# Two products of one weight tile in one 512-column matmul, in the memory stage of a decoder layer

## The chip, the cores and the metric

The program runs on one core of one Trainium2 chip. The time is device time in microseconds (us), from launch to end. Five engines with queues of their own matter: PE (TensorE, matrix multiply; its weight loads are shown as PEld), ACT (ScalarE), DVE (VectorE), POOL (GpSimd) and SP, which issues most DMAs. Each queue is worked off in the order in which the program was written out. Matmuls write into PSUM banks of 512 columns of 32 bits.

## The reference

One decoder layer on 512 tokens of width 2048: token mixing (retention and sliding-window attention), cross-attention into 256 memory tokens, gated MLP, each followed by a layer norm of the scaled residual sum. Only the cross-attention matters here:

```python
def memory_cross_attention(x, mem, wq, wkv, wo):
    q = (x @ wq).reshape(B, S, XA_HEADS, XA_HD)          # 4 heads of 512
    k, v = jnp.split(mem @ wkv, 2, axis=-1)              # 256 memory tokens
    logits = jnp.einsum('bshd,bmhd->bhsm', q, k) * XA_HD ** -0.5
    p = jax.nn.softmax(logits, axis=-1)
    return jnp.einsum('bhsm,bmhd->bshd', p, v).reshape(B, S, D_MODEL) @ wo
```

## The kernel before

All values are 32-bit floats. Each matrix is split into a high part and a low part (`split`: ACT casts the high part, DVE subtracts it to get the low part), and each product is made of three matmuls that add into one bank: high by high, low by high, high by low (`mm3`, lines 96 to 98).

The stage `memory()` comes first in the program and needs only the memory tokens and weights. Since keys and values are small, it folds them into the weights beside them. For each of four heads it runs

- `proj` twice: keys and values of the head, four weight chunks each. A chunk (1 MB, 128 rows by 2048 columns) is loaded into `raw` by a DMA on SP, split in two halves of 1024 columns into `whi` and `wlo` (four buffers each, so two chunks), and 16 weight tiles of each chunk multiply the memory tokens (`mh`, `ml`, 256 columns each) into a bank `psW`. The bank is split into `kvh` and `kvl`.
- the loop over `fq`: four chunks of `xa_q`, 16 tiles each, multiply the keys into banks `psT`. Eight tiles of a half chunk fill one bank (two results of 256 columns side by side), and ACT copies the whole bank to `ao`, which a DMA writes to a scratch tensor.
- `as_block`: four chunks of `xa_o` are multiplied by tiles of the values, into banks `psA` and `psB`; DVE copies them to `oo`.

There are two banks of each of the four kinds. A tile that takes a buffer over waits for the last reader of the tile that had it. The order of the instructions on each engine is not that of the source: a scheduler orders them when the program is built and writes one list for each engine. Two lines set what the change touches:

```python
def split(self, hi, lo, src, eng=None):
    self.nc.scalar.copy(hi, src)
    (eng or self.nc.vector).tensor_tensor(lo, src, hi.bitcast(F32), op=ALU.subtract)
```

Of the kernel before, what the change touches and what calls it, by code (L numbers as in the profile page):

```python
# [10 lines left out]
F32 = mybir.dt.float32  # L11
F32R = mybir.dt.float32r
AF = mybir.ActivationFunctionType
ALU = mybir.AluOpType
# [3 lines left out]
P = 128  # L18
D = 2048
S = 512  # L20
ML = 256
KT = D // P
# [14 lines left out]
class Layer:  # L37
# [128 lines left out]
    def memory(self):  # L166
        nc, I = self.nc, self.I
        with ExitStack() as c:
            mp = self.pool(c, "mem")
            mh = [mp.tile([P, 4, ML], F32R, name=f"mh{g}") for g in range(4)]  # L170
            ml = [mp.tile([P, 4, ML], F32R, name=f"ml{g}") for g in range(4)]
            ms = lambda k, cc: (mh[k // 4][:, k % 4, cc], ml[k // 4][:, k % 4, cc])
            stage = lambda: mp.tile([P, 2048], F32, name=self.n("stg"), tag="stg", bufs=2)
            raws = [stage() for _ in range(2)]
            first = self.st.tile([P, 2048], F32, name=self.n("raw"), tag="raw", bufs=3)

            def piece(i):
                k = slice(2 * i, 2 * i + 2)
                r = raws[i // 4].rearrange("p (k s) -> p k s", k=8)[:, 2 * i % 8:2 * i % 8 + 2]
                nc.sync.dma_start(r, I["memT"][:, k, :])  # L180
                kk = slice(2 * i % 4, 2 * i % 4 + 2)
                self.split(mh[i // 2][:, kk], ml[i // 2][:, kk], r)

            pre = []
            for h in range(2):
                piece(4 * h)
                c = slice(h * 1024, (h + 1) * 1024)
                nc.sync.dma_start(first[:, c], I["xa_k"][0][:, c])
                hi, lo = self.halves()
                self.split(hi, lo, first[:, c])  # L190
                pre.append((hi, lo))
                for i in range(1, 4):
                    piece(4 * h + i)
            def proj(name, h, pre=None):
                hi = mp.tile([P, 4, ML], F32R, name=self.n("kvh"), tag="kvh", bufs=2)
                lo = mp.tile([P, 4, ML], F32R, name=self.n("kvl"), tag="kvl", bufs=2)
                for q in range(4):
                    if pre and q == 0:
                        ps = self.bank("W")
                        self.ws_mm(ps, pre, ms, slice(0, ML))  # L200
                    else:
                        ps = self.ws(I[name][4 * h + q], ms, ML)
                    self.split(hi[:, q], lo[:, q], ps[:, :ML])
                return lambda k, cc: (hi[:, k, cc], lo[:, k, cc])

            self.swa_tables(mp)
            for h in range(XH):
                ks = proj("xa_k", h, pre if h == 0 else None)
                vs = proj("xa_v", h)
                if h == 1:  # L210
                    for g in range(4):
                        r = stage().rearrange("p (k s) -> p k s", k=4)
                        nc.sync.dma_start(r, I["xT"][:, 4 * g:4 * g + 4, :])
                        self.split(self.ah[g], self.al[g], r)
                for fq in range(4):
                    o = mp.tile([P, 4, ML], F32, name=self.n("ao"), tag="ao", bufs=2)
                    for hf, (hi, lo) in enumerate(self.chunk(I["xa_q"][4 * h + fq])):
                        ps = self.bank("T")
                        for i in range(2):
                            for k in range(4):  # L220
                                c = slice((4 * i + k) * P, (4 * i + k + 1) * P)
                                self.mm3(ps[:, i * ML:(i + 1) * ML], (hi[:, c], lo[:, c]), ks(k, slice(0, ML)),
                                         k == 0, k == 3)
                        nc.scalar.copy(o[:, 2 * hf:2 * hf + 2], ps.rearrange("p (i m) -> p i m", i=2))
                    nc.sync.dma_start(self.asc[h // 2][fq][:, :, h % 2 * ML:(h % 2 + 1) * ML], o)
                if h == 0:
                    self.swa_spread()
                for cb in range(4):
                    def done(m, a):
                        o = mp.tile([P, S], F32, name=self.n("oo"), tag="oo", bufs=2)  # L230
                        nc.vector.tensor_copy(o, a)
                        k = 2 * h + m
                        nc.sync.dma_start(self.osc[cb][k // 4][:, k % 4], o)

                    self.as_block([I["xa_o"][4 * h + cb]], vs, 512, 2, done, 4, "AA" if cb % 2 else "BB")


    def swa_tables(self, mp):
# [675 lines left out]
```

## Time and profile before

| | |
|---|---|
| runs | 2770.05, 2772.43, 2772.47 us; median 2772.43 us |
| profiled execution, its own time | 2770.75 us |
| its span, first to last instruction | 2769.0 us, so 1.75 us lie around it |
| PE busy | 2724.3 us, 98% of the span, 14402 matmuls |
| weight loads (PEld) | 85%, DVE 59%, ACT 34%, POOL 9% |
| granted clock | 0.993 of full speed on average |

The memory stage is the first 383 us or so. A matmul's busy time overlaps that of the next one, so the step from one matmul's start to the next one's is the measure of what it costs, and an idle time in front of one says what PE waited for.

### The profile page before, as it was taken

The page shows a single profiled execution, that of the slowest core. Times are in us where ns is not written, and L with a number is a line of the kernel's source. Part 1 is how long each engine was busy: PE and PEld are TensorE (multiplying, and loading weights), DVE is VectorE, ACT ScalarE, POOL GpSimd, SP SyncE. Part 2 cuts the span into 40 slices and gives each one's busy share as a digit, 9 for nine tenths or more (in the row PEclk, how much of TensorE's full clock was granted, in tenths as well). Part 3 has the DMA queues.
Part 4 walks back from the last instruction along what each step waited for, and adds up shares of the span by engine and source line. Part 5 has one row for each costly group of instructions (what it writes and reads, how often), then busy time and mean ns, then how long its engine had stood idle before and what let it go on. Part 6 is the DMA issues. An engine that isn't in the chain of part 4 may idle for free.

```text
span 2769.0 us, 35144 instructions
## 1 busy us (share of the span) xinstructions
PE 2724.3 (98%) x14402; PEld 2348.0 (85%) x14402; DVE 1635.8 (59%) x2344; ACT 945.6 (34%) x1304; POOL 262.1 (9%) x244
## 2 busy tenths in 40 slices
PE   8999999999999999999999999999999999999997
PEld 7999988898989988978888888888888888888876
DVE  6554545675344434554667667666666766666677
ACT  5444434442212322322433333333333333333331
POOL 0000001222111000260450000000000000000003
PEclk9999999999999999999999999999999999999998
DMA  8776672323222343132232223332223233322331
GB/s 320 244 243 208 226 232 79 95 74 97 99 88 96 122 152 125 43 126 93 95 111 98 103 92 107 107 107 92 97 102 107 92 106 107 107 100 99 107 122 61
DMA packets 70178, 337.68 MB, mean 122 GB/s; under 512 B 7504, under 2 KB 22272, under 8 KB 33536
## 3 DMA queue, kind: packets, MB, share of 16 engines
q1 hardware_dynamic: 63168, 320.89, 33.8%
q10 hardware_dynamic: 6848, 14.54, 1.6%
q8 instruction: 113, 1.85, 0.3%
q14 instruction: 49, 0.40, 0.1%
HBM read 311.27 MB, written 26.23 MB: 122 GB/s over the span
## 4 chain that ended last, share of the span: by engine, by line
PE 61%; DVE 2%; POOL 1%; ACT 0%; issue 0%; DMA 0%; DVEq 0%; ACTq 0%; POOLq 0%
PE psT L97 6%; PE psT L96 6%; PE psT L98 6%; PE psW L97 6%; PE psW L98 6%; PE psW L96 6%; PE psA L96 5%; PE psA L98 5%; PE psA L97 5%; PE psB L98 4%; PE psB L96 4%; PE psB L97 4%; PE psT L497 0%; POOL y L461 0%; DVE y L632 0%
## 5 line engine op out<-in xcount | busy, mean ns | idle before, releaser
L74 DVE TENSOR_TENSOR wlo<-raw,whi 128x1024 fp32r<-128x1024 f32 x512 | 643.8, 1260 | 848.2 <-ACT whi L73 846.9
L73 ACT CAST whi<-raw 128x1024 fp32r<-128x1024 f32 x512 | 537.4, 1051 | 1269.5 <-PE psW L97 572.6
L96 PE MATMUL psW<-ah,whi 128*128 128x512 f32 (+1 forms) x1136 | 443.3, 390 | 0.7 <-ACT ah L73 0.7
L98 PE MATMUL psW<-ah,wlo 128*128 128x512 f32 (+1 forms) x1136 | 442.1, 389 | 0.0
L97 PE MATMUL psW<-al,whi 128*128 128x512 f32 (+1 forms) x1136 | 441.3, 388 | 0.0
L96 PE MATMUL psT<-ah,whi 128*128 128x512 f32 (+1 forms) x720 | 276.7, 384 | 0.0
L97 PE MATMUL psT<-al,whi 128*128 128x512 f32 (+1 forms) x720 | 276.7, 384 | 0.0
L98 PE MATMUL psT<-ah,wlo 128*128 128x512 f32 (+1 forms) x720 | 276.7, 384 | 0.0
L96 PEld LDWEIGHTS psW<-ah,whi 128*128 128x128 f32 x1136 | 214.5, 189 | 44.1 <-ACT ah L73 1.2
L97 PEld LDWEIGHTS psW<-al,whi 128*128 128x128 f32 x1136 | 214.5, 189 | 43.7 <-issue 0.6
L96 PE MATMUL psA<-whi,ah 128*128 128x256 f32 (+1 forms) x800 | 245.8, 308 | 5.6 <-ACT xp L525 3.0
L98 PEld LDWEIGHTS psW<-ah,wlo 128*128 128x128 f32 x1136 | 214.6, 189 | 42.4
L97 PE MATMUL psA<-wlo,ah 128*128 128x256 f32 (+1 forms) x800 | 245.0, 306 | 0.0
L98 PE MATMUL psA<-whi,al 128*128 128x256 f32 (+1 forms) x800 | 244.8, 306 | 0.0
L96 PEld LDWEIGHTS psA<-whi,ah 128*128 128x128 f32 x800 | 153.7, 192 | 13.7 <-ACT xp L525 3.4
L97 PEld LDWEIGHTS psA<-wlo,ah 128*128 128x128 f32 x800 | 153.8, 192 | 6.6
L98 PEld LDWEIGHTS psA<-whi,al 128*128 128x128 f32 x800 | 153.7, 192 | 6.5
L98 PEld LDWEIGHTS psT<-ah,wlo 128*128 128x128 f32 x720 | 135.3, 188 | 26.8
L96 PEld LDWEIGHTS psT<-ah,whi 128*128 128x128 f32 x720 | 135.3, 188 | 26.8
L97 PEld LDWEIGHTS psT<-al,whi 128*128 128x128 f32 x720 | 135.3, 188 | 26.8
L96 PE MATMUL psW<-mh,whi 128*128 128x256 f32 x512 | 146.1, 285 | 3.0 <-ACT whi L73 3.0
L98 PE MATMUL psW<-mh,wlo 128*128 128x256 f32 x512 | 146.0, 285 | 2.3 <-DVE wlo L74 2.3
(307 smaller groups left out, 4759.6 us busy)
## 6 DMA issues: line engine op xcount, KB each, us to landing
raw<-in_ffn_up SPq DMA_DIRECT2D x88, 1024.0 KB, 4.9
raw<-in_w_in SPq DMA_DIRECT2D x44, 1024.0 KB, 5.0
raw<-in_ffn_down SPq DMA_DIRECT2D x44, 1024.0 KB, 4.9
raw<-in_xa_v SPq DMA_DIRECT2D x16, 1024.0 KB, 5.2
raw<-in_xa_q SPq DMA_DIRECT2D x16, 1024.0 KB, 4.9
raw<-in_xa_o SPq DMA_DIRECT2D x16, 1024.0 KB, 5.9
raw<-in_w_o SPq DMA_DIRECT2D x16, 1024.0 KB, 4.9
raw<-in_xa_k SPq DMA_DIRECT2D x15, 1024.0 KB, 7.1
```

Of the source, the lines that this page charges most:

```text
L73: self.nc.scalar.copy(hi, src)
L74: (eng or self.nc.vector).tensor_tensor(lo, src, hi.bitcast(F32), op=ALU.subtract)
L96: mm(ps, a[0], b[0], start=start, stop=False)
L97: mm(ps, a[0], b[1], start=False, stop=False)
L98: return mm(ps, a[1], b[0], start=False, stop=stop)
```

## The change

High and low parts lie side by side in one tile (`mt` for the memory tokens, `kv` for keys and values, 2 by 256 columns). A weight tile's high part multiplies both by one matmul of 512 columns, and its low part multiplies the high part by one of 256 columns. So the bank's left half holds two of the three products, its right half the third, and `both` adds the halves: ACT copies the right half to SBUF, DVE adds the left one to it. In `proj` the sum goes to a new tile `kt` before it is split. In the `fq` loop one result now fills a bank, so that a bank changes after 8 matmuls (4 tiles), where it changed after 24 (8 tiles).

```diff
-            mh = [mp.tile([P, 4, ML], F32R, name=f"mh{g}") for g in range(4)]
-            ml = [mp.tile([P, 4, ML], F32R, name=f"ml{g}") for g in range(4)]
+            mt = [mp.tile([P, 4, 2, ML], F32R, name=f"mt{g}") for g in range(4)]
+            ms = lambda k: mt[k // 4][:, k % 4]
...
+            def wide(ps, hi, lo, m, start, stop):
+
+                nc.tensor.matmul(ps, hi, m.rearrange("p i m -> p (i m)"), start=start, stop=False)
+                nc.tensor.matmul(ps[:, :ML], lo, m[:, 0], start=False, stop=stop)
+
+            def both(out, ps):
+
+                nc.scalar.copy(out, ps[:, ML:])
+                nc.vector.tensor_tensor(out, ps[:, :ML], out, op=ALU.add)
...
+                    hv = pre if pre and q == 0 else self.chunk(I[name][4 * h + q])
+                    ps = self.bank("W")
+                    for k in range(KT):
+                        hi, lo = hv[k // 8]
+                        w = slice((k % 8) * P, (k % 8 + 1) * P)
+                        wide(ps, hi[:, w], lo[:, w], ms(k), k == 0, k == KT - 1)
+                    t = mp.tile([P, ML], F32, name=self.n("kt"), tag="kt", bufs=2)
+                    both(t, ps)
+                    self.split(kv[:, q, 0], kv[:, q, 1], t)
...
                     for hf, (hi, lo) in enumerate(self.chunk(I["xa_q"][4 * h + fq])):
-                        ps = self.bank("T")
                         for i in range(2):
+                            ps = self.bank("T")
                             for k in range(4):
                                 c = slice((4 * i + k) * P, (4 * i + k + 1) * P)
-                                self.mm3(ps[:, i * ML:(i + 1) * ML], (hi[:, c], lo[:, c]), ks(k, slice(0, ML)),
-                                         k == 0, k == 3)
-                        nc.scalar.copy(o[:, 2 * hf:2 * hf + 2], ps.rearrange("p (i m) -> p i m", i=2))
+                                wide(ps, hi[:, c], lo[:, c], ks[:, k], k == 0, k == 3)
+                            both(o[:, 2 * hf + i], ps)
```

The scheduler's lists move with it. In the `fq` loop of the first head, ACT's list before alternates the cast of a weight half (L73, `whi`) and the copy of a whole bank (L224); the number behind a name only tells one tile from another.

```order
L73 CAST whi_778<-raw_776 128x1024
L224 COPY ao_647<-psT_658 128x512
L73 CAST whi_782<-raw_776 128x1024
L224 COPY ao_647<-psT_684 128x512
L73 CAST whi_842<-raw_840 128x1024
L224 COPY ao_711<-psT_722 128x512
L73 CAST whi_846<-raw_840 128x1024
```

ACT's list of the changed kernel at the same place (L200 is the copy in `both`; 540 and 544, 596 and 600 are the weight halves of the loop's first two chunks, 652 and 656, 708 and 712 those of the next two; the banks are filled in the order 548, 559, 570, 581, 604, 615, 626, 637):

```order
L200 COPY ao_537<-psT_548 128x256
L73 CAST whi_652<-raw_650 128x1024
L200 COPY ao_537<-psT_559 128x256
L73 CAST kv_344<-kt_532 128x256
L200 COPY ao_537<-psT_570 128x256
L73 CAST whi_656<-raw_650 128x1024
L200 COPY ao_537<-psT_581 128x256
L200 COPY ao_593<-psT_604 128x256
L73 CAST whi_708<-raw_706 128x1024
L200 COPY ao_593<-psT_615 128x256
```

The cast of a half still stands ahead of the copy of the bank that is finished at the same time, and there are now two copies, one for each bank, between two casts.

DVE's list before holds nothing of the `fq` loop's banks at this place, only the low parts of weights (L74):

```order
L74 TENSOR_TENSOR kvl_402<-psW_586,kvh_401 128x256
L74 TENSOR_TENSOR wlo_779<-raw_776,whi_778 128x1024
L74 TENSOR_TENSOR wlo_783<-raw_776,whi_782 128x1024
L74 TENSOR_TENSOR wlo_843<-raw_840,whi_842 128x1024
L74 TENSOR_TENSOR wlo_847<-raw_840,whi_846 128x1024
```

DVE's list of the changed kernel at the same place (L201 is the add in `both`):

```order
L74 TENSOR_TENSOR wlo_653<-raw_650,whi_652 128x1024
L201 TENSOR_TENSOR ao_537<-psT_559,ao_537 128x256
L74 TENSOR_TENSOR kv_344<-kt_532,kv_344 128x256
L201 TENSOR_TENSOR ao_537<-psT_570,ao_537 128x256
L74 TENSOR_TENSOR wlo_657<-raw_650,whi_656 128x1024
L201 TENSOR_TENSOR ao_537<-psT_581,ao_537 128x256
L201 TENSOR_TENSOR ao_593<-psT_604,ao_593 128x256
L74 TENSOR_TENSOR wlo_709<-raw_706,whi_708 128x1024
L201 TENSOR_TENSOR ao_593<-psT_615,ao_593 128x256
```

An add of 256 columns for each bank has come in, and the one of every second bank (559, 581, 615) stands behind a subtraction for a weight half. Behind the memory stage the lists of all engines are the same as before.

## Rows read from the trace of the kernel before

**Rows 1.** The page: span, and busy us (share) and instructions of each engine.
```profile
span 2769.0 us, 35144 instructions
...
PE 2724.3 (98%) x14402; PEld 2348.0 (85%) x14402; DVE 1635.8 (59%) x2344; ACT 945.6 (34%) x1304; POOL 262.1 (9%) x244
```

**Rows 2.** Busy us by stretch: PE, PEld, DVE, ACT, POOL, granted clock, DMA share, GB/s.
```profile
0.00:20.00 20.00, 10.03 (x53) 8.13 (x54) 9.35 (x13) 10.61 (x15) 0.74 (x7) 1.00 0.87 311
20.00:400.00 380.00, 375.52 (x2763) 357.00 (x2764) 198.91 (x199) 166.61 (x197) 0.21 (x1) 1.00 0.72 246
```

**Rows 3.** What PE waited for, 0 to 460 us: total us, times, longest.
```profile
PE psW L96 <- ACT whi L73: 3.0, 3, 1.4
PE psA L96 <- DVE oo L231: 2.3, 1, 2.3
PE psW L98 <- DVE wlo L74: 2.3, 3, 0.8
```

**Rows 4.** PE in time, psA's and psW's matmuls: start us, us.
```profile
102.14 0.39 PE L96 MATMUL psA<-whi,kvh 128*128 128x512 f32 x1
...
107.50 0.40 PE L98 MATMUL psA<-whi,kvl 128*128 128x512 f32 x1
107.74 0.28 PE L96 MATMUL psW<-mh,whi 128*128 128x256 f32 x1
...
124.29 0.28 PE L96 MATMUL psW<-mh,whi 128*128 128x256 f32 x1
```

**Rows 5.** PE in time, first and later matmul of the fq loop.
```profile
62.72 0.28 PE L96 MATMUL psT<-kvh,whi 128*128 128x256 f32 x1
...
68.14 0.28 PE L97 MATMUL psT<-kvl,whi 128*128 128x256 f32 x1
```

**Rows 6.** PE in time, 512 columns by a weight tile, in the MLP.
```profile
1601.06 0.39 PE L97 MATMUL psT<-al,whi 128*128 128x512 f32 x1
...
1605.14 0.39 PE L97 MATMUL psT<-al,whi 128*128 128x512 f32 x1
```

**Rows 7.** ACT in time, in the fq loop.
```profile
68.46 1.05 ACT L73 CAST whi<-raw 128x1024 fp32r<-128x1024 f32 x1 [1.29 <-PE psT L97]
69.41 0.58 ACT L224 COPY ao<-psT 128x512 f32<-128x512 f32 x1
```

**Rows 8.** DVE in time, start of the program and of the fq loop.
```profile
13.11 1.23 DVE L74 TENSOR_TENSOR wlo<-raw,whi 128x1024 fp32r<-128x1024 f32 x1 [1.76 <-ACT whi L73]
...
63.88 1.23 DVE L74 TENSOR_TENSOR wlo<-raw,whi 128x1024 fp32r<-128x1024 f32 x1 [1.66 <-ACT whi L73]
65.03 0.42 DVE L74 TENSOR_TENSOR kvl<-psW,kvh 128x256 fp32r<-128x256 f32 x1
...
69.54 1.23 DVE L74 TENSOR_TENSOR wlo<-raw,whi 128x1024 fp32r<-128x1024 f32 x1 [1.60 <-ACT whi L73]
```

**Rows 9.** ACT by line, 0 to 460 us: 256 columns from a bank, mean ns.
```profile
L73 ACT CAST kvh<-psW 128x256 fp32r<-128x256 f32 x32 | 11.8, 368 | 5.8 <-PE psW L98 5.8
```

**Rows 10.** PE in time, waits of the start and of the stage's end.
```profile
14.39 0.39 PE L98 MATMUL psW<-mh,wlo 128*128 128x256 f32 x1 [0.76 <-DVE wlo L74]
...
32.81 0.38 PE L96 MATMUL psW<-mh,whi 128*128 128x256 f32 x1 [1.41 <-ACT whi L73]
...
383.47 0.36 PE L96 MATMUL psA<-whi,ah 128*128 128x256 f32 x1 [2.31 <-DVE oo L231]
...
384.06 0.41 PE L96 MATMUL psA<-whi,ah 128*128 128x256 f32 x1
384.27 0.41 PE L97 MATMUL psA<-wlo,ah 128*128 128x256 f32 x1
```

**Rows 11.** Busy us by stretch, columns as in rows 2, around two of these waits.
```profile
28.00:36.00 8.00, 5.84 (x47) 5.43 (x46) 5.77 (x6) 6.52 (x7) 0.00 (x0) 1.00 0.97 396
...
383.70:387.10 3.40, 3.40 (x18) 3.40 (x18) 1.44 (x2) 0.00 (x0) 0.00 (x0) 0.50 0.98 340
```

More of the change, by code (lines that the diff above doesn't have):

```diff
@@ L169, in memory @@
             mp = self.pool(c, "mem")
-            mh = [mp.tile([P, 4, ML], F32R, name=f"mh{g}") for g in range(4)]
-            ml = [mp.tile([P, 4, ML], F32R, name=f"ml{g}") for g in range(4)]
-            ms = lambda k, cc: (mh[k // 4][:, k % 4, cc], ml[k // 4][:, k % 4, cc])
+            mt = [mp.tile([P, 4, 2, ML], F32R, name=f"mt{g}") for g in range(4)]
+            ms = lambda k: mt[k // 4][:, k % 4]
             stage = lambda: mp.tile([P, 2048], F32, name=self.n("stg"), tag="stg", bufs=2)
@@ L181, in piece @@
                 kk = slice(2 * i % 4, 2 * i % 4 + 2)
-                self.split(mh[i // 2][:, kk], ml[i // 2][:, kk], r)
+                self.split(mt[i // 2][:, kk, 0], mt[i // 2][:, kk, 1], r)
             pre = []
@@ L193, in memory @@
                     piece(4 * h + i)
+            def wide(ps, hi, lo, m, start, stop):
[4 more added lines that the diff above has]
+                nc.vector.tensor_tensor(out, ps[:, :ML], out, op=ALU.add)
             def proj(name, h, pre=None):
-                hi = mp.tile([P, 4, ML], F32R, name=self.n("kvh"), tag="kvh", bufs=2)
-                lo = mp.tile([P, 4, ML], F32R, name=self.n("kvl"), tag="kvl", bufs=2)
+                kv = mp.tile([P, 4, 2, ML], F32R, name=self.n("kv"), tag="kv", bufs=2)
                 for q in range(4):
[L198 to L204, printed above, removed]
+                    hv = pre if pre and q == 0 else self.chunk(I[name][4 * h + q])
[7 more added lines that the diff above has]
+                    self.split(kv[:, q, 0], kv[:, q, 1], t)
+                return kv
             self.swa_tables(mp)
@@ L233, in done @@
                         nc.sync.dma_start(self.osc[cb][k // 4][:, k % 4], o)
-                    self.as_block([I["xa_o"][4 * h + cb]], vs, 512, 2, done, 4, "AA" if cb % 2 else "BB")
+                    self.as_block([I["xa_o"][4 * h + cb]], lambda k, cc: (vs[:, k, 0, cc], vs[:, k, 1, cc]), 512, 2, done, 4, "AA" if cb % 2 else "BB")
     def swa_tables(self, mp):
```

## The prediction

> **What bounds the kernel now.** I read the page first: PE is busy for 2724 of 2769 us [rows 1]. Then the stretches: after a start in which data is still arriving, PE works 375.5 of 380 us of the memory stage, with DVE at 199, ACT at 167 and the DMA engines at 0.72 [rows 2]. The list of waits says the same: up to the end of the stage PE waits three times for a cast, three times for a low part and once for a copy, 7.6 us in all [rows 3]. So whatever shortens PE's own stream counts in full, and so does every new wait of PE. The last view is PE in order of time, for the step from one matmul to the next.
>
> **What the matmuls cost.** 256 columns step by 16.55 us over 138 matmuls, 0.120 us, in `proj` [rows 4], and by 5.42 us over 46, 0.118 us, in the `fq` loop [rows 5]. 512 columns step by 5.36 us over 23, 0.233 us, where the stationary tiles are values [rows 4], and by 4.08 us over 18, 0.227 us, where they are weight tiles as in the changed kernel [rows 6]. Three matmuls of 256 thus cost 0.360 us (0.353 in the `fq` loop), and the new pair 0.227 + 0.120 = 0.347 us (0.345): twice the columns cost 7 to 13 ns less than two matmuls of half the size, and only that is won, since the columns that stream are the same 768. `proj` has 512 such triples (4 heads, 8 chunks, 16 tiles), the `fq` loop 256: 512 x 13 ns + 256 x 8.5 ns = **8.8 us gained**. Bounds: with 0.233 for the wide one, 512 x 7 + 256 x 2 ns = 4 us. At the other end a wide one and a narrow one each 2 to 4 ns below the quickest step of rows 5 and 6 would give 12 us. I take 8.8, since the row that it rests on has the same roles of the operands.
>
> [...] The sum goes by the rows.
>
> At the start PE waits for loads: the waits up to 32.81 us end when a weight half has arrived [rows 3, 10]. What the first three chunks gain before that is waited for instead, 48 triples x 13 ns = **0.6 us lost**.
>
> **What the evictions cost.** `proj` adds 32 copies (0.37 us, as the cast of 256 columns from a bank [rows 9]) and 32 adds (0.42 us, as the `kvl` subtraction, which also reads a bank and an SBUF tile [rows 8]). The `fq` loop gets 64 copies of 0.37 for 32 of 0.58 [rows 7] and 64 new adds of 0.42. That is 17 us more of ACT and 40 us more of DVE, on engines that are idle for 213 and 181 us of the stage [rows 2]. In `proj` the two `psW` banks change only every 16 x 0.347 = 5.55 us, which hides copy, add and split even behind a cast and a subtraction. The keys are needed four chunks later, the values more than three. The scratch write on SP now waits for DVE instead of ACT, and the loads of `xa_o` that it used to stand among have been moved ahead of it. These edits I cost at nothing.
>
> The `psT` banks are another matter. A bank is filled in 4 x 0.345 = 1.38 us, there are two, and a third result needs the first one's bank back. Take a half chunk with banks X and Y, and let t be the moment at which PE is through with Y and could go on. The weight half is free too at that moment, and ACT's list has the cast into it (652) ahead of the copy of Y (559); DVE's list has the subtraction ahead of the add of Y. So:
>
> - The last matmul on the high part started 0.345 us before t and is shown for 0.39 us. ACT starts 0.04 us behind its end (68.14 + 0.28 to 68.46 [rows 5, 7]): cast from t + 0.08 to t + 1.13.
> - DVE starts 0.03 us behind that (68.46 + 1.05 to 69.54 [rows 7, 8]), at t + 1.16. DVE's next instruction starts 1.15 us after the subtraction (63.88 to 65.03 [rows 8]): the add of Y from t + 2.31 to t + 2.73. The copy of Y is done by t + 1.5 and waits for nobody.
> - PE starts 0.05 us behind DVE (13.11 + 1.23 to 14.39 [rows 8, 10]): t + 2.78. In between it has only the next half's X, until t + 1.38.
>
> PE waits **1.40 us for each half chunk**, and then the same begins again: a period of 4.16 us instead of 2.76. The first half waits as long, in two pieces: a cast and the last values' add stand ahead of the first bank, 0.37 us, and then Y, 1.03 us. I went through the lists of all four heads, which repeat. In each, four half chunks have this wait. After the eleventh bank the scheduler has placed 12, 24, 24 and 12 matmuls of `xa_o` between the banks, 2.8 us or more at 0.233 us, and they cover the rest; the first 12 wait for a low part made behind the same cast: it is there at t + 2.39 + 0.05, while PE has work for 1.38 + 2 x 0.233 us, so 0.6 us. Per head 4 x 1.40 + 0.6 = 6.2 us, **25.0 us in all**. Bounds: if the subtraction holds DVE for its full 1.23 us, 1.48 us a wait, 26 us. If each link is 0.05 us shorter, 1.25 us a wait, 22 us.
>
> **Sum**, on the profiled execution (span 2769.0, 2770.75 with what lies around it): 2770.75 - 8.8 + 0.6 + 25.0 = 2787.6 us. The median of the runs is 1.7 us above that execution: **2789 us**, 0.6% slower. With the bounds, 2782 to 2796.
>
> **The rivals.** A change within 0.2%, 5.5 us, can't be told from none here.
>
> - *The bank is returned in time* (the other side: faster). If ACT and DVE took Y's copy and add ahead of the cast and the subtraction, Y would be free at t + 0.16 + 0.04 + 0.37 + 0.03 + 0.42 + 0.05 = t + 1.07, before the next X is through at t + 1.38. It decides at 1.38 us. Then only the gain stays, 2772.4 - 8.8 + 0.6 = 2764 us. Against it stands the printed order, and that a cast of the loop did start at once behind its half's last use [rows 5, 7], so that it will be in the way. Chance 0.08.
> - [...] Chance 0.05.
> - *The clock falls in the loop.* [...] From 28 to 36 us, where PE was idle for 2.16 us, 1.41 of it in one wait, it stayed at 1.00 [rows 10, 11]. [...] Chance 0.08.
> - *Something else*, such as a load that comes late in the moved order: 0.04.
>
> **How the numbers follow.** The forecast has the remaining 0.75 and 2782 to 2796 as its own range. Cases on both sides together hold 0.25, so the range reaches part of the way to each: 2777 to 2803. Faster by over 0.2%: 0.08. Within 0.2%: 0.07 (the bare rate, and a part of the waits only). Slower by over 0.2%: 0.85.
>
> **What would show it.** PE in order of time: a pair of 512 and 256 columns should step by 0.347 us in `proj`. The list of waits: a new row, `psT` behind DVE's add, about 20 times and 22 us in all (16 waits of 1.4 us in four heads, four of them in two pieces), and `psB` behind a low part, 4 times 0.6 us. ACT in order of time: a cast between the copies of X and Y. The stage's last matmul on `psA` should end some 17 us later than at 381, and what follows should take as long as before. The prediction is wrong if the pair steps below 0.33 us, if there is no wait on `psT`, or if the clock row shows 0.50 in the `fq` loop.

## The result, and the profile after

Slower, by about as much as forecast. The changed kernel takes 2792.73 us in the median of 4 runs (2791.24 to 2796.38), the kernel before 2771.24 us of 4 beside it: ratio 1.0082, 95% interval 1.007 to 1.0094, 21.5 us. The forecast was 2789 us, 16.6 us over the median that it started from. The profiled execution is the slowest of the four, 2796.38 us, so the trace explains 25.6 us between the two profiled executions and not 21.5.

The page after, first and third line (answers to [rows 1]): 768 matmuls fewer, PE busy as before, and 25.6 us more span.

```profile
span 2794.6 us, 33781 instructions
...
PE 2726.5 (98%) x13634; PEld 2307.8 (83%) x13634; DVE 1667.4 (60%) x2440; ACT 960.3 (34%) x1368; POOL 260.6 (9%) x244
```

Busy us by stretch of the kernel after, columns as in [rows 2]. PE works 355.1 of 380 us where it worked 375.5. The line from 28 us answers to [rows 11]. That from 33.6 us is a stretch at the start with PE at a granted clock of 0.51; the last lies in the `fq` loop.

```profile
20.00:400.00 380.00, 355.14 (x1853) 297.32 (x1852) 221.13 (x284) 175.43 (x255) 0.00 (x0) 0.99 0.67 228
28.00:36.00 8.00, 3.83 (x18) 2.76 (x17) 5.44 (x7) 5.02 (x8) 0.00 (x0) 0.85 1.00 402
33.60:40.50 6.90, 5.65 (x16) 4.46 (x17) 5.99 (x6) 5.38 (x5) 0.00 (x0) 0.51 0.99 393
...
66.00:80.00 14.00, 10.52 (x55) 8.20 (x55) 7.84 (x13) 6.67 (x13) 0.00 (x0) 1.00 0.50 159
```

What PE waited for after, 0 to 480 us (answers to [rows 3]). The row on `ao` is new and holds two thirds of these; that on `psB` is new too. The row on `whi` has a longest wait of 3.7 us where it had 1.4.

```profile
PE psT L195 <- DVE ao L201: 18.8, 20, 1.3
...
PE psW L195 <- ACT whi L73: 4.3, 2, 3.7
PE psA L96 <- DVE oo L241: 2.4, 1, 2.4
PE psW L196 <- DVE wlo L74: 2.0, 3, 0.8
PE psB L97 <- DVE wlo L74: 1.9, 4, 0.5
```

The `fq` loop after on PE in order of time (answers to [rows 5]), around one of these waits:

```profile
71.93 0.40 PE L195 MATMUL psT<-kv,whi 128*128 128x512 f32 x1
...
72.63 0.40 PE L195 MATMUL psT<-kv,whi 128*128 128x512 f32 x1
...
73.69 0.40 PE L195 MATMUL psT<-kv,whi 128*128 128x512 f32 x1
73.92 0.28 PE L196 MATMUL psT<-kv,wlo 128*128 128x256 f32 x1
75.46 0.51 PE L195 MATMUL psT<-kv,whi 128*128 128x512 f32 x1 [1.26 <-DVE ao L201]
75.81 0.28 PE L196 MATMUL psT<-kv,wlo 128*128 128x256 f32 x1
```

The same moment on ACT (answers to [rows 7]), and under it on DVE (answers to [rows 8]). The cast stands before the copies, the subtraction before the adds. "x2" is two instructions in one row, the adds of two banks.

```profile
72.77 1.05 ACT L73 CAST whi<-raw 128x1024 fp32r<-128x1024 f32 x1 [2.04 <-PE psT L195]
73.72 0.36 ACT L200 COPY ao<-psT 128x256 f32<-128x256 f32 x1
74.24 0.37 ACT L200 COPY ao<-psT 128x256 f32<-128x256 f32 x1 [0.16 <-PE psT L196]
```

```profile
73.85 1.23 DVE L74 TENSOR_TENSOR wlo<-raw,whi 128x1024 fp32r<-128x1024 f32 x1 [2.12 <-ACT whi L73]
74.99 0.75 DVE L201 TENSOR_TENSOR ao<-psT,ao 128x256 f32<-128x256 f32 x2
```

Read from PE to PE, with the forecast's t, which is 72.63 here: bank Y is full, PE begins to fill the other bank, and ACT and DVE have been idle (2.04 and 2.12 us in front of these rows). But they turn to the weights first: cast at t + 0.14, subtraction at t + 1.22. Only at t + 2.36 (74.99) does DVE add Y, and PE, which issued its last matmul for the other bank at 73.92, goes on at t + 2.83 (75.46); the forecast had t + 2.78. An ordinary step is 0.12 us, so the step of 1.54 from 73.92 holds 1.42 us of wait: 1.26 us shown as idle, and 0.16 us in which the matmul before is still shown as busy. The forecast was 1.40.

`proj` on PE, in the first head and in the second (answers to [rows 4]): 16 pairs in 5.55 us, 0.347 us each, and 15 pairs in 5.29 us, 0.353 us each.

```profile
41.20 0.39 PE L195 MATMUL psW<-mt,whi 128*128 128x512 f32 x1
...
46.75 0.39 PE L195 MATMUL psW<-mt,whi 128*128 128x512 f32 x1
...
118.94 0.40 PE L195 MATMUL psW<-mt,whi 128*128 128x512 f32 x1
...
124.23 0.40 PE L195 MATMUL psW<-mt,whi 128*128 128x512 f32 x1
```

The start and the end of the stage on PE (answers to [rows 10]):

```profile
30.40 0.28 PE L196 MATMUL psW<-mt,wlo 128*128 128x256 f32 x1
34.39 0.80 PE L195 MATMUL psW<-mt,whi 128*128 128x512 f32 x1 [3.71 <-ACT whi L73]
35.65 0.58 PE L196 MATMUL psW<-mt,wlo 128*128 128x256 f32 x1 [0.46 <-DVE wlo L74]
...
410.29 0.36 PE L96 MATMUL psA<-whi,ah 128*128 128x256 f32 x1 [2.35 <-DVE oo L241]
```

The wait of 3.71 us is one that the forecast did not have. ACT of the kernel after, ahead of it:

```profile
27.16 1.91 ACT L73 CAST ah<-stg 128x2048 fp32r<-128x2048 f32 x1 [5.11 <-DMA stg<-in_xT]
28.97 0.36 ACT L200 COPY kt<-psW 128x256 f32<-128x256 f32 x1
31.76 0.40 ACT L73 CAST kv<-kt 128x256 fp32r<-128x256 f32 x1 [2.43 <-DVE kt L201]
32.07 0.36 ACT L200 COPY kt<-psW 128x256 f32<-128x256 f32 x1
32.98 0.40 ACT L73 CAST kv<-kt 128x256 fp32r<-128x256 f32 x1 [0.55 <-DVE kt L201]
33.30 1.99 ACT L73 CAST whi<-raw 128x1024 fp32r<-128x1024 f32 x2
```

And DVE of the kernel after, there:

```profile
29.09 2.29 DVE L74 TENSOR_TENSOR al<-stg,ah 128x2048 fp32r<-128x2048 f32 x1 [5.54 <-ACT ah L73]
31.30 0.42 DVE L201 TENSOR_TENSOR kt<-psW,kt 128x256 f32<-128x256 f32 x1
```

ACT of the kernel before, at the same point of its list:

```profile
31.44 0.37 ACT L73 CAST kvh<-psW 128x256 fp32r<-128x256 f32 x1 [1.48 <-PE psW L98]
31.71 1.99 ACT L73 CAST whi<-raw 128x1024 fp32r<-128x1024 f32 x2
```

Before, ACT casts the key bank from PSUM as soon as PE has filled it, and needs nothing of DVE. Now the sum of the two halves is made by DVE, which is busy with a low part of `x` (`al`, 2.29 us); ACT waits 2.43 and 0.55 us for it, and the 4th chunk's casts, behind that in ACT's list, start 1.59 us later than before.

From the first matmuls of each part in the trace, profiled executions after against before: first head's keys and values 57.62 us (from 7.85 to 65.47) against 54.90; keys and values of the other three heads 45.22 against 46.07 each; the `fq` and `xa_o` parts 26.6 us more in all (51.7 against 45.0 in the first head); so the stage ends 26.8 us later, at 410.29, and what follows takes 1.2 us less.

### The profile page after: what moved, and what is told of

It is laid out like the page before. It is cut to its first block, busy times and chain, and to the rows that moved or that the text cites. A ratio compares the mean times of both kernels' runs of the same rounds, so it can differ in the third digit from the quotient of the medians.

```text
span 2794.6 us, 33781 instructions
## 1 busy us (share of the span) xinstructions
PE 2726.5 (98%) x13634; PEld 2307.8 (83%) x13634; DVE 1667.4 (60%) x2440; ACT 960.3 (34%) x1368; POOL 260.6 (9%) x244
## 4 chain that ended last, share of the span: by engine, by line
PE 61%; DVE 2%; ACT 0%; issue 0%; DMA 0%; POOL 0%; DVEq 0%; ACTq 0%
PE psT L97 6%; PE psT L96 6%; PE psT L98 6%; PE psW L97 6%; PE psW L98 6%; PE psW L96 6%; PE psA L96 5%; PE psA L97 5%; PE psA L98 5%; PE psB L96 4%; PE psB L97 4%; PE psB L98 4%; PE psT L507 0%; DVE y L642 0%; PE psT L543 0%
## 5 line engine op out<-in xcount | busy, mean ns | idle before, releaser
L74 DVE TENSOR_TENSOR wlo<-raw,whi 128x1024 fp32r<-128x1024 f32 x512 | 642.3, 1257 | 836.8 <-ACT whi L73 835.0
L73 ACT CAST whi<-raw 128x1024 fp32r<-128x1024 f32 x512 | 537.6, 1052 | 1271.9 <-PE psW L97 491.0
L195 PE MATMUL psW<-mt,whi 128*128 128x512 f32 x512 | 185.5, 405 | 4.3 <-ACT whi L73 4.3
L96 PEld LDWEIGHTS psT<-ah,whi 128*128 128x128 f32 x720 | 135.3, 188 | 26.8
L98 PEld LDWEIGHTS psT<-ah,wlo 128*128 128x128 f32 x720 | 135.3, 188 | 26.8
L97 PEld LDWEIGHTS psT<-al,whi 128*128 128x128 f32 x720 | 135.3, 188 | 26.8
L196 PE MATMUL psW<-mt,wlo 128*128 128x256 f32 x512 | 146.2, 286 | 2.0 <-DVE wlo L74 2.0
```

The source lines that it names most:

```text
L96: mm(ps, a[0], b[0], start=start, stop=False)
L97: mm(ps, a[0], b[1], start=False, stop=False)
L98: return mm(ps, a[1], b[0], start=False, stop=stop)
L195: nc.tensor.matmul(ps, hi, m.rearrange("p i m -> p (i m)"), start=start, stop=False)
L196: nc.tensor.matmul(ps[:, :ML], lo, m[:, 0], start=False, stop=stop)
```

## The experiments

Each ran on one chip beside the kernel before. Medians in us, ratios to the kernel before with their 95% intervals:

| kernel | time | before there | ratio |
|---|---|---|---|
| four_banks | 2770.81 | 2770.7 | 0.9998 (0.9989 to 1.0007) |
| evict_first | 2769.67 | 2770.7 | 0.9996 (0.9987 to 1.0005) |
| proj_only | 2771.05 | 2770.7 | 0.9999 (0.9989 to 1.0008) |
| old_small_banks | 2770.87 | 2770.7 | 1.0001 (0.9992 to 1.0011) |
| four_start | 2770.81 | 2771.12 | 0.9999 (0.999 to 1.0008) |
| evict_start | 2772.18 | 2771.12 | 1.0004 (0.9996 to 1.0013) |
| proj_start | 2773.41 | 2771.12 | 1.0007 (0.9998 to 1.0015) |
| fq_only | 2798.63 | 2771.12 | 1.0098 (1.0082 to 1.0113) |
| late_proj | 2765.29 | 2771.89 | 0.998 (0.9971 to 0.9989) |
| late_four | 2765.53 | 2771.89 | 0.998 (0.9971 to 0.9989) |
| early_proj | 2772.21 | 2771.89 | 1.0005 (0.9996 to 1.0014) |

**Are the waits on the second bank the loss?** First, two more banks for the loop (`psW` is idle there):

```diff
-                            ps = self.bank("T")
+                            ps = self.bank("TW"[i])
```

> The changed kernel, but in the fq loop the second result of each half chunk goes to a psW bank, which is free there, so that four banks take turns. Theory (PE waits for the second bank of a half, held up behind a cast on ACT and a subtraction on DVE): with four banks each is needed only 4.1 us after it was filled, more than the 2.78 us of the chain, so the 20 waits of PE on DVE's add vanish and about 25 us with them: 2768 us, 0.1 to 0.2% under the kernel before. Rival (the additional copies and adds cost as such, or the wide pair itself is slow, or the clock): 2785 us or more, waits or long steps remain.

What PE waited for in this kernel, 0 to 460 us. The row on `ao` is gone, and the `fq` and `xa_o` parts take 45.0 us a head again.

```profile
PE psW L195 <- ACT whi L73: 4.4, 2, 4.1
PE psA L96 <- DVE oo L241: 2.6, 1, 2.6
PE psW L196 <- DVE wlo L74: 1.7, 3, 0.8
```

Second, two banks as in the change, but the weight half's cast and subtraction stand behind the copy and add of the bank that is finished at that moment (`after` holds them for each half):

```diff
+            with ExitStack() as st:
+                for i in (after[h] if after else ()):
+                    st.enter_context(self.tc.issue_after(i.ins))
-            self.split(hi, lo, raw[:, h * 1024:(h + 1) * 1024])
+                self.split(hi, lo, raw[:, h * 1024:(h + 1) * 1024])
```

> The changed kernel with the same instructions, two banks, but the cast and the subtraction for a weight half are put behind the copy and the add of the bank that is finished at the same moment. Theory (it is the order in the queues): the second bank of a half comes back in 1.07 us and has no wait; but now the subtraction stands ahead of the first bank's add, which ends at about 3.15 us where PE needs it at 2.76 us: a wait of about 0.4 us for each half in place of 1.4 us, 2775 to 2781 us. Rival (two banks of 1.38 us are too few whatever the order): as slow as the changed kernel, 2790 us or more.

ACT of this kernel in the loop: copy, copy, cast.

```profile
71.82 0.37 ACT L203 COPY ao<-psT 128x256 f32<-128x256 f32 x1 [0.24 <-PE psT L199]
73.22 0.37 ACT L203 COPY ao<-psT 128x256 f32<-128x256 f32 x1 [1.03 <-PE psT L199]
73.49 1.05 ACT L73 CAST whi<-raw 128x1024 fp32r<-128x1024 f32 x1
```

PE waits four times on `ao`, 0.7 us in all, and the loop's head takes 46.3 us, 1.3 more than before the change. So the order in two queues, not the number of banks as such, made the 1.4 us waits: either remedy takes back the whole loss. It came out better than I had expected: 2775 to 2781 us were forecast.

**Which half of the change holds the loss?** The wide pair in `proj` alone, and in the `fq` loop alone (the other part as before the change):

```diff
# proj_only: the fq loop
+                        ps = self.bank("T")
                         for i in range(2):
-                            ps = self.bank("T")
...
-                                wide(ps, hi[:, c], lo[:, c], ks[:, k], k == 0, k == 3)
-                            both(o[:, 2 * hf + i], ps)
+                                self.mm3(ps[:, i * ML:(i + 1) * ML], (hi[:, c], lo[:, c]), (ks[:, k, 0], ks[:, k, 1]), k == 0, k == 3)
+                        nc.scalar.copy(o[:, 2 * hf:2 * hf + 2], ps.rearrange("p (i m) -> p i m", i=2))
# fq_only: proj
-                        wide(ps, hi[:, w], lo[:, w], ms(k), k == 0, k == KT - 1)
-                    t = mp.tile([P, ML], F32, name=self.n("kt"), tag="kt", bufs=2)
-                    both(t, ps)
-                    self.split(kv[:, q, 0], kv[:, q, 1], t)
+                        self.mm3(ps[:, :ML], (hi[:, w], lo[:, w]), (ms(k)[:, 0], ms(k)[:, 1]), k == 0, k == KT - 1)
+                    self.split(kv[:, q, 0], kv[:, q, 1], ps[:, :ML])
```

> The wide pair in the projections of keys and values alone, the fq loop as before with banks of 24 matmuls. Theory: no waits in the fq loop; 512 triples gain 7 to 8 ns each (pairs of 0.352 us as in the changed kernel), 4 us, and the start loses 1 to 5 us: 2768 to 2773 us, same as before. Rival (copy, add and split in the projections cost more than they hide): 2778 us or more.

> The wide pair in the fq loop alone, proj's banks split as before the change. Theory: the waits on the second bank stay (idle 1.25 us, 18 to 20 us over four heads), the start is that of the kernel before, and the time is 2790 to 2796 us, of the size of the whole change's loss. Rival (the loss comes from proj's copies and adds in the same queues): under 2780.

The loss is in the loop: `fq_only` is 27 us slower, more than the whole change and 2.6 us above the range expected, with the same row in its list of waits, 0 to 460 us:

```profile
PE psT L195 <- DVE ao L201: 18.3, 20, 1.2
```

`proj_only` is no faster than before in the median, although its heads 2 to 4 take 44.4 us for keys and values where 46.07 stood, 5.1 us in all. Its first head's take 56.6, so 1.7 us of this go there. The profile does not show where the rest goes: the stage ends 4.3 us earlier than before (379.14), but that execution, 2766.49 us, is the fastest of the ten.

**Does one result per bank cost by itself?** The kernel before, with its three matmuls and one copy of 256 columns per bank:

```diff
-                        ps = self.bank("T")
                         for i in range(2):
+                            ps = self.bank("T")
...
-                        nc.scalar.copy(o[:, 2 * hf:2 * hf + 2], ps.rearrange("p (i m) -> p i m", i=2))
+                            nc.scalar.copy(o[:, 2 * hf + i], ps[:, :ML])
```

> The kernel before with its three matmuls, but one result a bank in the fq loop: a bank changes after 12 matmuls (1.41 us), and ACT alone evicts it, with a copy of 256 columns. Theory (DVE's subtraction and add make most of the wait): the chain is cast and copy alone, 1.46 us against 1.41 us that PE has, so about 0.05 us for each half: 2772 us, the same as before. Rival (changing the bank every 1.4 us is slow in itself, or the cast alone makes the wait): 2782 us or more.

The loop's head takes 45.5 us, 0.5 more: the copy behind the cast costs 0.14 us a half chunk. With one engine in the chain the small banks are all but harmless; with ACT and then DVE, each behind its own long instruction, they cost 1.4.

**Where does `proj`'s gain go?** My theory was the start: a wait of some 4 us (3.71 in the changed kernel) and the granted clock of 0.51 behind it. A first remedy put the copies, adds and splits of the first head's keys behind the splits of the chunks that follow, and the splits of `x` into the second head's keys; it was tried with four banks, with the order of `evict_first`, and with `proj` alone:

```diff
...
+                    if pre and q < 2:
+                        ahead += [self.chunk(I[name][j]) for j in ((1,), (2, 3))[q]]
+                        self.third = self.last_split
+                    with ExitStack() as st:
+                        if pre:
+                            for i in self.third:
+                                st.enter_context(self.tc.issue_after(i.ins))
-                    both(t, ps)
-                    self.split(kv[:, q, 0], kv[:, q, 1], t)
+                        both(t, ps)
+                        self.split(kv[:, q, 0], kv[:, q, 1], t)
...
+                        with self.tc.issue_after(self.gate[0].ins), self.tc.issue_after(self.gate[1].ins):
-                        self.split(self.ah[g], self.al[g], r)
+                            self.split(self.ah[g], self.al[g], r)
```

> The changed kernel with the fq loop alternating over the banks psT and psW (no waits on the second bank's add), and besides, at the start, ACT and DVE serve the 2nd to 4th weight chunk of the first head's keys ahead of the copies and adds of the banks that finish meanwhile, and the splits of x (four casts and subtractions of 2048 columns) come behind the second head's keys, so that the 4th chunk's cast waits for nothing but its DMA. Theory (the gain of the wide pair in proj, four times 1.7 us, was given back by the wait of about 4 us and the half clock behind it at the start): the wait on the 4th chunk's cast falls to 1.5 us or less, no stretch at .50 behind it, the first head's keys and values take 53.5 to 55 us where they took 58.1, and the time is 2764 to 2767 us, 0.15 to 0.25% under the kernel before. Rival (the wait at the start is set by the DMA and not by ACT's order): wait and clock dip stay, 2769 to 2772.

> As the run before, but with two banks psT only and the copies and adds ahead of the weight halves' casts and subtractions in the fq loop. Theory: start as in the run before, the remaining short waits of .3 us a half cost 1.2 us a head, so 2766 to 2770. Rival: 2769 to 2772, the wait at the start stays.

> The wide pair in proj alone (fq loop as before the change), with the order at the start as in the two runs before. Theory: 2764 to 2767, as with four banks, since the fq loop's pair gives nothing. Rival (the fq loop's wide pair does gain when it has no wait): 1 to 3 us slower than with four banks.

All three missed in time. In `four_start` the first head's keys and values did fall to 54.2 us, as expected, but the second head's rose to 48.7 (47.0 and 48.5 in the other two). PE there, behind the moved splits of `x`, waits and then steps slowly (0.59 and 0.21 us where 0.23 and 0.12 are usual):

```profile
126.58 0.80 PE L196 MATMUL psW<-mt,whi 128*128 128x512 f32 x1 [2.50 <-DVE kt L202]
127.17 0.42 PE L197 MATMUL psW<-mt,wlo 128*128 128x256 f32 x1
127.38 0.63 PE L196 MATMUL psW<-mt,whi 128*128 128x512 f32 x1
```

In the other two the long wait at the start stayed as well (4.59 and 3.98 us, now for the bank). ACT of `evict_start`:

```profile
31.41 1.99 ACT L73 CAST whi<-raw 128x1024 fp32r<-128x1024 f32 x2 [8.15 <-DMA raw<-in_xa_k]
33.30 0.64 ACT L204 COPY kt<-psW 128x256 f32<-128x256 f32 x2
```

The remedy had put a bank's return behind a load, which came late: the old fault again, in a new place. It could not tell the theory from its rival, so the next three leave the start alone. `late_proj` and `late_four` (as `proj_only` and `four_banks`) compute the first head's keys as before the change; `early_proj` has the wide pair there and nowhere else (the condition turned round).

```diff
+                        if pre:
+                            self.mm3(ps[:, :ML], (hi[:, w], lo[:, w]), (ms(k)[:, 0], ms(k)[:, 1]), k == 0, k == KT - 1)
+                        else:
-                        wide(ps, hi[:, w], lo[:, w], ms(k), k == 0, k == KT - 1)
+                            wide(ps, hi[:, w], lo[:, w], ms(k), k == 0, k == KT - 1)
+                    if pre:
+                        self.split(kv[:, q, 0], kv[:, q, 1], ps[:, :ML])
+                        continue
...
```

> The wide pair in proj alone and there not in the first head's keys, which are computed and split as before the change; the fq loop as before the change. Theory (proj's pair saves 0.85 us per pass of four chunks, and only the first head's keys give it back by the longer wait on the 4th chunk and the half clock behind it): first head's keys and values 54 us, the other heads' 44.4, and the time 7 times 0.85 = 5.9 us under the kernel before, 2765 to 2768. Rival (what proj saves is given back behind the memory stage or lost in the executions' own spread): 2770 to 2772, with the memory stage's end still 5 to 6 us earlier in the profile.

> The changed kernel with four banks in the fq loop and the first head's keys computed and split as before the change. Theory: as the run before, 2764 to 2768 (in the fq loop the wide pair without its waits gives nothing). Rival: 2770 to 2772.

> The wide pair in the first head's keys alone, all else as before the change. Theory: the wait on the 4th chunk is about 4 us where it was 1.4, a stretch of half clock stands behind it, the first head's keys and values take 57 to 58.5 us (54.9 before), and the time is 2 to 4 us above the kernel before, 2773 to 2775. Rival (the start's wait does not last to the end): 2770 to 2772.

Both `late` kernels beat the kernel before, by 5.5 us (3.0 to 8.0) as the ratios have it and by 6.6 and 6.4 in the medians, where 5.9 was expected. PE of `late_proj`: the second head's keys and values from 107.75 to 152.13, 44.38 us or 0.3467 us a pair; the stage ends at 377.79, 5.7 us earlier than before [rows 10].

```profile
107.75 0.40 PE L195 MATMUL psW<-mt,whi 128*128 128x512 f32 x1
...
152.13 0.28 PE L96 MATMUL psT<-kv,whi 128*128 128x256 f32 x1
...
377.79 0.36 PE L96 MATMUL psA<-whi,ah 128*128 128x256 f32 x1 [1.70 <-DVE oo L248]
```

And what it waited for, 0 to 460 us: the longest wait for a cast is again that of [rows 3]. But its first head's keys and values took 55.1 us, not 54, and those of `late_four` 57.0: in both the granted clock fell at the start, to 0.86 from 30 to 42 us, though the keys are computed as before the change.

```profile
PE psW L96 <- ACT whi L73: 1.8, 2, 1.4
```

```profile
30.00:42.00 12.00, 9.84 (x63) 9.20 (x62) 10.16 (x10) 8.91 (x10) 0.00 (x0) 0.86 1.02 425
```

`late_four` is as fast as `late_proj`: without its waits the loop's wide pair neither gains nor loses. `early_proj` does not decide: 58.8 us for the first head's keys and values in its profile, and a wait of 2.36 us where I expected about 4, but a time below the 2773 to 2775 us forecast, and a ratio whose interval holds both my 2 to 4 us and nothing.

So it is shown that the gain of `proj` reaches the total when the first head's keys are left alone, in two pairs of kernels (`late_proj` against `proj_only`, `late_four` against `four_banks`), 5 us each by the ratios. Why it is 5 us is not shown. With the wide pair in the first head's keys, its keys and values took 56.6 to 59.3 us in five profiles (58.1 on average), with the old form and order 54.9 to 57.9 in five others (56.0). That is some 2 us of the 5, and 2.4 if the 0.85 us are put back that the values gain where they have the pair too.

## Why the prediction was right

- **The waits on the second bank.** Right in place, mechanism and size. The step of 1.54 us holds 1.42 us where 1.40 was worked out, link by link as forecast, 12 times; the first half of each head waits in two pieces, as forecast, 0.2 and 0.75 to 0.81 us idle, 1.25 to 1.3 us by steps. The `xa_o` wait is 0.47 us idle, 0.63 with the 0.16 us in which the matmul before is still shown as busy (forecast 0.6). All in all the `fq` and `xa_o` parts take 26.6 us more, forecast 25.0 for the waits (4 heads of 6.2 us are 24.8, a slip without weight). What is beyond that is of the size of a step that I had not priced: the first wide matmul behind a wait takes 0.33 to 0.35 us to the next (75.46 to 75.81) where 0.23 is usual, at each of the 20 waits. That this is the loss is shown by `four_banks` and `evict_first`, which remove it in different ways, and by `fq_only`, which has nothing else.
- **The pair.** 0.347 us in the first head's `proj`, as forecast; but 0.353 in the other three heads of this kernel, so that they gave 0.85 us each instead of 1.66. In the `fq` loop it is also 0.353 (71.93 to 73.69, 5 pairs), the price of the three that it replaced: forecast 2.2 us of gain, measured none. So the gain of 8.8 us was put too high: the trace shows 2.6 in heads 2 to 4, 1.7 in the first head (given back there, see below) and none in the loop. Why the same `proj` matmuls step by 0.347 us in heads 2 to 4 of the eight experiments that have the pair there, and by 0.353 here, stays open.
- **The start, the step that failed.** "These edits I cost at nothing" was wrong for the first head's keys. I looked at the `psW` banks and at when the keys are needed, but not at what stands behind the copies in ACT's list while DVE holds them up: the casts of a chunk that PE is waiting for. Forecast for the first head's keys and values: 1.66 gained, 0.6 of it given back, so 1.06 us less. Measured 2.72 us more. Of these, 1.55 us stand when the fourth chunk begins, 34.39 against 32.81 us, after starts at 7.85 and 7.82: the wait in front of it is 2.3 us longer, 0.7 of it because PE comes to it earlier, 1.6 because ACT's casts come later. The other 1.17 us arise behind it. The first nine pairs (34.39 to 40.50) run at a granted clock of 0.51 (33.6 to 40.5 us) and take 5.65 us beside a wait of 0.46, where nine at 0.347 us take 3.1: 2.5 us lost, of which the pair's gain in five chunks (1.1 us) and a wait for a low part shorter by 0.3 us give back 1.4.
- **The load that the start waits for.** The 0.6 us lost came out, as the 0.7 just named, but by luck: the reading behind it was wrong. Before, the cast that ends the wait at 32.81 starts (31.71) right behind the cast of the third key bank, which had waited 1.48 us for PE: that wait was set by ACT's list already, not by a load. `late_proj` and `old_small_banks` have the same 1.41 us there. The prediction's 7.6 us of waits also leave out the first one, 6.9 us for a load, which both kernels have.
- **How sure the start's price is.** The 2.72 us rest on one profile of each kernel, and that of the kernel before was a lucky one: its clock did not fall there, as it did in three of the other four profiles with the old form and order. Over five profiles each the difference is some 2 us. `late_proj` against `proj_only` gives 5.3 us by the ratios and 7.0 by the medians; what of the stage their two profiles show is 1.4 us. So that the first head's keys are the place is shown by the times, the delay of the casts by the rows above; the rest of the 5 us stays open.
- **The sum.** For the `fq` and `xa_o` parts, the first head's keys and values and those of the other heads the forecast had +22.8, -1.1 and -5.0 us, 16.8 in all; the trace has +26.6, +2.7 and -2.6, 26.8 in the stage, and -1.2 behind it. So every part came out dearer. That the medians are 21.5 us apart and not 25.6 lies in the profiled executions: that of the kernel after is 3.65 us above its median, that of the kernel before 0.5 below. The time came out within the range because the term that decides it was right; the smaller terms were not.
- **The rivals.** The bank was not returned in time; `evict_first` shows that the order decides it, as that rival had it. No run shows the bare rate that is part of the 0.07 within 0.2%; the pair stepped by 0.347 and 0.353 us. The clock did not fall in the loop: the granted clock is 1.00 from 66 to 80 us, over four waits on `psT` of 0.17 to 1.26 us idle, and in the loops of all four heads. It did fall at the start (0.51 from 33.6 to 40.5 us), where I had no rival.

## What to carry to other kernels

Where the eviction was split over two engines here, its price was not the two instructions (0.37 and 0.42 us) but what stood ahead of them in each engine's list when the bank was full, added up: a cast of 1.05 and a subtraction of 1.23 us, in a loop that fills the other bank in 4 pairs of 0.353 us, and the wait was 1.42 us. Add it up in the same way and compare it with the time in which the other bank is filled. Then look the other way too: what stands behind the new instructions, and which of it is something that PE waits for. A gain of a few nanoseconds a matmul (0.347 us for a pair where three took 0.360) was worth having only where both answers were harmless: doing it there alone (`late_proj`, ratio 0.998) beat doing it everywhere (1.0082).

## What the runs showed of the hardware

The clock's fall at the start does not follow from the length of a wait alone. The kernel before waited 1.41 and 0.76 us in a row and kept 1.00 [rows 10, 11]. `late_proj` had the same two waits and 0.86. `old_small_banks` has the same instructions there and the same two waits, and its granted clock was 0.86 from 30 to 42 us and 0.92 ahead of that; its first head's keys and values took 57.9 us against 54.9:

```profile
8.00:30.00 22.00, 19.22 (x121) 18.32 (x122) 12.01 (x16) 10.94 (x14) 0.00 (x0) 0.92 0.99 374
30.00:42.00 12.00, 9.83 (x68) 9.43 (x67) 9.92 (x9) 7.00 (x7) 0.00 (x0) 0.86 1.01 414
```

So some 3 us lie between two executions in their first 42 us, with the same instructions there, and one profile of the start does not give its mean price. At the stage's end it was the other way round: a wait of 2.31 us was followed by 0.50 before [rows 10, 11], and one of 2.35 us by 1.00 after, in steps of 0.12 us (410.72 to 414 us). What follows the stage, which none of these kernels changes, took 2382.5 to 2389.3 us in the 13 profiles, more apart than most of the differences above.

The clock column does not fit the steps in the first microseconds: from 9 to 11 us of the kernel before it says 1.00, while the matmuls of 256 columns step by 0.21 us, as they do at 0.50 [rows 10, 11].
